# The low parts of the weights: one place modulo 512 bytes in the feature-major product, another in the token-major one

## The chip, the cores and the metric

The kernel runs on one core of one Trainium2 chip. The metric is the device time of one execution in microseconds (us). Before the change it is 2848.39 us, the median of 3 runs (2848.35 to 2848.42).

## The reference

A two-layer network over one sequence of 256 tokens with 2048 features, in float32. Layer 0 mixes tokens with a gated recurrence (HGRN2, 8 heads) and with low-rank attention (MLA, 8 heads); layer 1 mixes with retention (8 heads of 256 by 512). After each mixer come a gated feed-forward part with a short convolution, and a gated embedding of a second input `p`. Cut to its frame:

```python
for i in range(DEPTH):                                   # 2
    u = rmsnorm(h, norm_mix[i])
    mix = even_mixer(u, ...) if i % 2 == 0 else odd_mixer(u, ...)
    h = h + mix
    h = h + conv_ffn(rmsnorm(h, norm_ffn[i]), w_gate, w_up, conv_w, conv_b, w_down)   # 2048 -> 5632 -> 2048
    gate = sigmoid(rmsnorm(h, norm_ple[i]) @ ple_w_gate[i])
    h = h + (p[i] @ ple_w_proj[i]) * gate
```

Nearly all the work is products of an activation of 256 tokens with float32 weight matrices, each of which is used once: about 520 MB of weights are read.

## The kernel before

**Two parts of a number.** The products are made in the type float32r. To keep float32's accuracy, each operand is split into a high part (rounded to float32r) and a low part (the remainder): weights into `wh` and `wl`, activations into the two halves of one tile `x` of 128 partitions by 512 numbers, `x[:, 0:256]` high and `x[:, 256:512]` low, for 256 tokens. A product is the sum of three: `wh` with x high, `wh` with x low, `wl` with x high.

**The weights' way.** A block of weights of 128 partitions by 1024 numbers (512 KB) comes by DMA into `raw` (line 153, 4 buffers). ScalarE rounds it into `wh` (line 158, 3 buffers); VectorE subtracts and writes `wl` (line 161, 4 buffers).

**The feature-major product**, `gemm_fm` (line 172): the output's features lie on the partitions. A slice of 128 by 128 weights is loaded into TensorE, and x streams past it: once for `wh` with both halves of x, 512 columns (line 184), once for `wl` with the high half, 256 columns (line 186). The weights of two blocks are taken together (`RUN = 2`): 16 matmuls with `wh`, then the 16 with `wl` for the same chunks. `gemm_fm1` (line 199) does the same in matmuls of 256 columns (lines 209, 211, 212), one after the other for each slice.

**The token-major product**, `gemm_tm` (line 217): tokens lie on the partitions. Here 128 by 128 numbers of x are loaded, and 512 columns of weights stream past: x high with `wh` (line 228), x high with `wl` (line 229), x low with `wh` (line 230), for two halves of the tokens. `first_values` (line 235) is the same for the first weights of the kernel (lines 263 to 265); its first two chunks have buffers of their own, `wh0` and `wl0`.

In both forms one operand stands still in the array (it is loaded by an instruction of its own, which the profile shows as PEld and which runs beside the matmul ahead of it), and the other streams. In the feature-major form the low part of a weight is loaded; in the token-major one it streams.

**Where tiles lie.** Pools hand out a partition's bytes in the order of allocation. A tile of 512 or 1024 numbers takes 2048 or 4096 bytes, so all buffers of one kind lie at the same place modulo 512, and so does each slice of 128 numbers within them. `shift` (line 141) puts a small unused tile ahead of a pool's tiles to move them. Before the change the x tiles of every stage, `raw` and `wh` lie at 64 modulo 512, and `wl`, behind a pad of `LOW_SHIFT` = 320 bytes, at 384. `wh0` and `wl0` of `first_values` lie at 0.

**Order.** Python generators (`spawn`, `pump`) interleave the small work of each stage with the products: a product's loop calls `pump()` after a block or two, which lets every waiting stage issue its next step. Each engine then runs its instructions in the order in which they were issued, and waits on semaphores where data or a buffer is missing.

**The rotary part of the queries** is one such stage: `q_rope` in `mla` (line 803) writes y (tag `ly`, 2 buffers), its square, y times a gain into `lyg` (line 810, 1 buffer), and `rotate` (line 769) multiplies that with a permutation on TensorE (line 772). It runs twice.

Of the kernel before, what the change touches and what calls it, by code (L numbers as in the profile page):

```python
# [8 lines left out]
F32 = mybir.dt.float32  # L9
F32R = mybir.dt.float32r  # L10
BF16 = mybir.dt.bfloat16
I32 = mybir.dt.int32
AF = mybir.ActivationFunctionType
# [4 lines left out]
P = 128  # L18
T = 256
# [5 lines left out]
F_HALVES = ((0, 24), (24, 44))  # L25
KB = 4
RUN = 2
LOW_SHIFT = 320
EPS = 1e-6

HG_HEADS = 8
# [47 lines left out]
def hybrid_kernel(ctx, tc, io):  # L79
    nc = tc.nc  # L80
# [4 lines left out]
    xpool = ctx.enter_context(tc.tile_pool(name="xpool", bufs=NX, reuse_waits="tile"))  # L85
    wpool = ctx.enter_context(tc.tile_pool(name="wpool", bufs=4))
# [18 lines left out]
    def vcol(name, i=0, n=1):  # L105
        if name == "mix0":
            return vec0[:, i:i + n]
        a = VEC[name][0] + i
        return vec[:, a:a + n]
# [7 lines left out]
    def pump():  # L117
        for g in active[:]:
            if next(g, active) is active:
                active.remove(g)  # L120
# [17 lines left out]

    shifted = set()

    def shift(pool, name, n):


        if name not in shifted:
            shifted.add(name)
            pool.tile([P, n // 4], F32, name=f"pad_{name}", bufs=1)

    def load_w(src, width):
        return split_w(fetch_w(src, width), width)

    def fetch_w(src, width):
        raw = wpool.tile([P, width], F32, tag="raw", name="raw", bufs=4)
        nc.sync.dma_start(out=raw, in_=src)
        return raw

    def split_w(raw, width):
        wh = wpool.tile([P, width], F32R, tag="wh", name="wh", bufs=3)
        nc.scalar.copy(wh, raw)  # L158
        shift(wpool, "wl", LOW_SHIFT)
        wl = wpool.tile([P, width], F32R, tag="wl", name="wl", bufs=RUN + 2)  # L160
        nc.vector.tensor_tensor(wl, raw, wh.bitcast(F32), op=ALU.subtract)  # L161
        return wh, wl

    def blocks_of(blocks, n, width, kb, sub=None):

        sub = sub or kb
        for k0 in range(0, n, sub):
            k1 = min(n, k0 + sub)
            o = (k0 % kb) * width
            yield range(k0, k1), load_w(blocks[k0 // kb][:, o:o + (k1 - k0) * width], (k1 - k0) * width)  # L170

    def gemm_fm(blocks, xs):

# [43 lines left out]
    def gemm_tm(blocks, xs, sub=None):  # L217

        ps = [psum.tile([P, 512], F32, tag="mm", name="mm", bufs=5) for _ in range(2)]
        n = len(xs)  # L220
        for ks, (wh, wl) in blocks_of(blocks, n, 512, 2, sub):
            for kc in ks:
                x = xs[kc]
                o = (kc - ks[0]) * 512
                for m in range(2):
                    xh = x[:, m * P:(m + 1) * P]
                    xl = x[:, T + m * P:T + (m + 1) * P]
                    nc.tensor.matmul(ps[m], xh, wh[:, o:o + 512], start=(kc == 0), stop=False)  # L228
                    nc.tensor.matmul(ps[m], xh, wl[:, o:o + 512], start=False, stop=False)  # L229
                    nc.tensor.matmul(ps[m], xl, wh[:, o:o + 512], start=False, stop=(kc == n - 1))  # L230
            if ks[-1] % 4 == 3:
                pump()
        return ps

    def first_values(src, xs):


        ps = [[psum.tile([P, 512], F32, tag="mm", name="mm", bufs=5) for _ in range(2)] for _ in range(2)]
        n = len(xs)
        with tc.tile_pool(name="first", bufs=4) as first:  # L240
            raws = {}

            def fetch(kc):
                if kc < 2:
                    for g in range(2):
                        raws[kc, g] = first.tile([P, 512], F32, tag="raw0", name="raw0")
                        nc.sync.dma_start(out=raws[kc, g], in_=src[kc][:, g * 512:(g + 1) * 512])
                elif kc < n:
                    raws[kc] = fetch_w(src[kc], 1024)

            def split_half(raw):
                wh = first.tile([P, 512], F32R, tag="wh0", name="wh0")
                nc.scalar.copy(wh, raw)
                wl = first.tile([P, 512], F32R, tag="wl0", name="wl0")
                nc.vector.tensor_tensor(wl, raw, wh.bitcast(F32), op=ALU.subtract)
                return wh, wl

            def products(kc, g, wh, wl, o):
                x = xs[kc]
                for m in range(2):  # L260
                    xh = x[:, m * P:(m + 1) * P]
                    xl = x[:, T + m * P:T + (m + 1) * P]
                    nc.tensor.matmul(ps[g][m], xh, wh[:, o:o + 512], start=(kc == 0), stop=False)  # L263
                    nc.tensor.matmul(ps[g][m], xh, wl[:, o:o + 512], start=False, stop=False)  # L264
                    nc.tensor.matmul(ps[g][m], xl, wh[:, o:o + 512], start=False, stop=(kc == n - 1))  # L265

            xs.fetch(0, 0)
            fetch(0)
            xs.fetch(0, 1)
            fetch(1)  # L270
            for i in range(1, 3):
                xs.fetch(i)
                fetch(2 * i)
                fetch(2 * i + 1)
            xs.fetch(3)
            for kc in range(n):
                if kc < 2:
                    for g in range(2):
                        products(kc, g, *split_half(raws[kc, g]), 0)
                else:  # L280
                    wh, wl = split_w(raws[kc], 1024)
                    for g in range(2):
                        products(kc, g, wh, wl, g * 512)
                    fetch(kc + 4)
                    if kc % 2 == 0 and kc // 2 + 3 < n // 2:
                        xs.fetch(kc // 2 + 3)
                if kc % 4 == 3:
                    pump()
        return ps
# [126 lines left out]
    rope_t = {}  # L416

    def rope_tables(tpool):
        posi = tpool.tile([P, T], I32, tag="posi", name="posi", bufs=1)
        nc.sync.dma_start(out=posi, in_=io["positions"])  # L420
        yield from steps(2)
        posf = tpool.tile([P, T], F32, tag="posf", name="posf", bufs=1)
        nc.vector.tensor_copy(posf, posi)
        for name in ("mla", "ret"):
            ang = tpool.tile([P, T], F32, tag="ang", name="ang", bufs=1)
            nc.vector.tensor_scalar(ang, posf, vcol(f"invf_{name}"), None, op0=ALU.mult)
            cs = cpool.tile([P, T], F32, name=f"cos_{name}")
            sn = cpool.tile([P, T], F32, name=f"sin_{name}")
            sin_of(sn, ang, 0.0, tpool)
            sin_of(cs, ang, 0.25, tpool)  # L430
            rope_t[name] = (cs, sn)
            yield


    def ffn_and_ple(i, st):
        rs = token_stats(st[0], D, 2)
        xs = st[1]
        cw, cb = f"cw{i}", f"cb{i}"
        st = new_norm()
        with tc.tile_pool(name=f"ffn{i}", bufs=2, reuse_waits="tile") as fp:  # L440
            silu = {}

            def gate(ps, f):
# [46 lines left out]
            xs = st[1]  # L490
# [174 lines left out]
    def even_mixer(rs, xs):  # L665
# [1 line left out]
        mix_a, mix_b = {}, {}  # L667
        first = first_values(io["w_hv"], xs)
        with tc.tile_pool(name="low", bufs=2) as low:
            shift(low, "low", 64)  # L670
            kpe = low.tile([P, 1, T], F32, name="kpe", bufs=1)
            with tc.tile_pool(name="l0a", bufs=2) as pool:
                hvs = {}
# [91 lines left out]
    def mla(pool, kpe, ckv, cq, rkv, rqa, mix, fill):  # L765
# [3 lines left out]
        def rotate(dst, y):  # L769
            ps = small([P, 2, T], "sm_rot")  # L770
            n = y.shape[1]
            nc.tensor.matmul(ps[:, 0:n], mcol("swap"), y, start=True, stop=True)
            mul(y, y, bcast(cos, n), nc.gpsimd)
            mul(dst, ps[:, 0:n], bcast(sin, n))
            nc.vector.tensor_tensor(dst, dst, y, op=ALU.add)
# [25 lines left out]
        qr, sqr, mv, pairs = {}, {}, {}, {}  # L801

        def q_rope(ps, g):
            yield from until(rqa, "bc")
            y = pool.tile([P, 2, T], F32, tag="ly", name="ly")
            mul(y, ps, bcast(rqa["bc"]))
            sq = pool.tile([P, 2, T], F32, name=f"sqr{g}", bufs=1)
            nc.scalar.activation(sq, y, AF.Square)
            yg = pool.tile([P, 2, T], F32, tag="lyg", name="lyg", bufs=1)
            nc.scalar.activation(yg, y, AF.Copy, scale=vcol("qr"))  # L810
            yield
            z = pool.tile([P, 2, T], F32, name=f"qr{g}", bufs=1)
            rotate(z, yg)
            for j in range(2):
                sqr[2 * g + j] = sq[:, j]
                qr[2 * g + j] = z[:, j]
# [111 lines left out]
    def odd_mixer(st):  # L928
        rs = token_stats(st[0], D, 2)
        xs = st[1]  # L930
        st = new_norm()
        cs, sn = rope_t["ret"]
        with tc.tile_pool(name="l1", bufs=1, reuse_waits="tile") as l1, \
                tc.tile_pool(name="l1t", bufs=2, reuse_waits="tile") as lt:
            shift(l1, "l1", 64)
            mx = {}
            rot = {}
            gates = {}
# [146 lines left out]
    xs = Arriving()  # L1085
# [120 lines left out]
```

## Time and profile before

| | |
|---|---|
| time, median of 3 runs | 2848.39 us |
| profiled execution, its own time | 2848.95 us |
| its span, first to last instruction | 2847.1 us |
| VectorE busy | 1898.6 us (67%) |
| ScalarE busy | 1403.0 us (49%) |
| DMA queue of the weights | 522.95 MB, 57.5% of 16 engines |

A row of the timeline gives the start in us from the span's start, the time to the end of the last instruction of the group, the engine (PE is TensorE's matmuls, PEld its weight loads), the line of the kernel, the operation, what it writes and reads, and after an x how many instructions stand in the group. Matmuls are pipelined: one starts long before the one ahead of it has ended. What a stream of them costs is therefore the **step**, from one start to the next start, and not the duration of one. A group's mean step is the start of the next group, less its own start, divided by its count.

### The profile page before, as it was taken

The page shows a single profiled execution, that of the slowest core. Times are in us where ns is not written, and L with a number is a line of the kernel's source. Part 1 is how long each engine was busy: PE and PEld are TensorE (multiplying, and loading weights), DVE is VectorE, ACT ScalarE, POOL GpSimd, SP SyncE. Part 2 cuts the span into 40 slices and gives each one's busy share as a digit, 9 for nine tenths or more (in the row PEclk, how much of TensorE's full clock was granted, in tenths as well). Part 3 has the DMA queues.
Part 4 walks back from the last instruction along what each step waited for, and adds up shares of the span by engine and source line. Part 5 has one row for each costly group of instructions (what it writes and reads, how often), then busy time and mean ns, then how long its engine had stood idle before and what let it go on. Part 6 is the DMA issues. An engine that isn't in the chain of part 4 may idle for free.

```text
span 2847.1 us, 41083 instructions
## 1 busy us (share of the span) xinstructions
PE 2838.5 (100%) x16025; PEld 2474.0 (87%) x16025; DVE 1898.6 (67%) x2753; ACT 1403.0 (49%) x1844; POOL 84.7 (3%) x123
## 2 busy tenths in 40 slices
PE   9999999999999999999999999999999999999999
PEld 7888888888888888888888888888888888888888
DVE  8776787766557776785555555556777755777666
ACT  6665555444344444564444444445444433444444
POOL 1110300000000000000000000000000000000000
PEclk9999999999999999999999999999999999999999
DMA  7555445556655665565555555555665655666564
GB/s 242 175 157 163 133 154 189 188 191 192 192 187 191 189 189 188 187 194 183 182 180 182 189 185 181 178 178 185 196 191 186 193 189 189 192 188 194 186 194 165
DMA packets 147939, 525.58 MB, mean 185 GB/s; under 512 B 16544, under 2 KB 18336, under 8 KB 147744
## 3 DMA queue, kind: packets, MB, share of 16 engines
q1 hardware_dynamic: 147600, 522.95, 57.5%
q8 instruction: 125, 2.05, 0.3%
q14 instruction: 70, 0.57, 0.1%
q10 hardware_dynamic: 144, 0.01, 0.0%
HBM read 520.80 MB, written 2.10 MB: 184 GB/s over the span
## 4 chain that ended last, share of the span: by engine, by line
PE 98%; DVE 1%; DMA 0%; POOL 0%; issue 0%; ACT 0%; SPq 0%; DVEq 0%
PE mm L184 52%; PE mm L186 27%; PE mm L230 4%; PE mm L229 4%; PE mm L228 4%; PE sm_ro L1008 1%; PE mm L209 1%; PE mm L212 1%; PE mm L211 1%; PE mm L264 0%; PE mm L265 0%; PE sm_ra L987 0%; PE mm L263 0%; DMA raw<-in_w_hv 0%; PE sm_sc L875 0%; DVE wl L161 0%
## 5 line engine op out<-in xcount | busy, mean ns | idle before, releaser
L161 DVE TENSOR_TENSOR wl<-raw,wh 128x1024 fp32r<-128x1024 f32 (+1 forms) x990 | 1200.4, 1219 | 819.3 <-ACT wh L158 801.6
L158 ACT CAST wh<-raw 128x1024 fp32r<-128x1024 f32 (+1 forms) x990 | 1032.0, 1043 | 1205.2 <-PE mm L184 776.7
L184 PE MATMUL mm<-xs,wh 128*128 128x512 f32 x4288 | 1028.8, 391 | 0.0
L184 PEld LDWEIGHTS mm<-xs,wh 128*128 128x128 f32 x4288 | 787.1, 188 | 153.1 <-DVE xs L311 0.4
L186 PEld LDWEIGHTS mm<-xs,wl 128*128 128x128 f32 x4288 | 541.2, 189 | 19.1
L186 PE MATMUL mm<-xs,wl 128*128 128x256 f32 x4288 | 550.5, 281 | 0.0
L184 PE MATMUL mm<-hs,wh 128*128 128x512 f32 x1408 | 337.2, 391 | 0.0
L184 PEld LDWEIGHTS mm<-hs,wh 128*128 128x128 f32 x1408 | 258.2, 188 | 49.6
L229 PE MATMUL mm<-wl,xs 128*128 128x512 f32 x512 | 202.0, 394 | 0.0
L230 PE MATMUL mm<-wh,xs 128*128 128x512 f32 x512 | 201.8, 394 | 0.0
L228 PE MATMUL mm<-wh,xs 128*128 128x512 f32 x512 | 201.7, 394 | 0.0
L186 PEld LDWEIGHTS mm<-hs,wl 128*128 128x128 f32 x1408 | 179.4, 189 | 7.3
L186 PE MATMUL mm<-hs,wl 128*128 128x256 f32 x1408 | 181.7, 281 | 0.0
L295 ACT COPY evt<-mm 128x256 f32<-128x256 f32 x300 | 98.2, 374 | 92.9 <-PE mm L186 92.9
L184 PE MATMUL mm<-xo,wh 128*128 128x512 f32 x512 | 122.7, 391 | 0.0
L230 PEld LDWEIGHTS mm<-wh,xs 128*128 128x128 f32 x512 | 96.2, 188 | 22.4
L229 PEld LDWEIGHTS mm<-wl,xs 128*128 128x128 f32 x512 | 96.1, 188 | 22.1
L228 PEld LDWEIGHTS mm<-wh,xs 128*128 128x128 f32 x512 | 96.2, 188 | 21.9
L184 PEld LDWEIGHTS mm<-xo,wh 128*128 128x128 f32 x512 | 94.0, 188 | 18.5 <-DVE xo L1025 0.3
L399 DVE TENSOR_TENSOR h<-h,mm 128x256 f32<-128x256 f32 x128 | 48.1, 415 | 35.7 <-PE mm L186 35.7
L186 PEld LDWEIGHTS mm<-xo,wl 128*128 128x128 f32 x512 | 64.9, 189 | 2.4
L186 PE MATMUL mm<-xo,wl 128*128 128x256 f32 x512 | 65.9, 281 | 0.0
(275 smaller groups left out, 1952.5 us busy)
## 6 DMA issues: line engine op xcount, KB each, us to landing
raw<-in_wg SPq DMA_DIRECT2D x176, 512.0 KB, 3.7
raw<-in_wu SPq DMA_DIRECT2D x176, 512.0 KB, 4.1
raw<-in_wd SPq DMA_DIRECT2D x176, 512.0 KB, 3.9
raw<-in_w_oqk SPq DMA_DIRECT2D x64, 512.0 KB, 4.2
raw<-in_w_ov SPq DMA_DIRECT2D x64, 512.0 KB, 3.7
raw<-in_w_og SPq DMA_DIRECT2D x64, 512.0 KB, 3.5
raw<-in_w_oo SPq DMA_DIRECT2D x64, 512.0 KB, 4.1
raw<-in_wpg SPq DMA_DIRECT2D x60, 512.0 KB, 3.6
```

Source lines behind the costliest of these rows:

```text
L158: nc.scalar.copy(wh, raw)
L161: nc.vector.tensor_tensor(wl, raw, wh.bitcast(F32), op=ALU.subtract)
L184: nc.tensor.matmul(ps[j], w[:, o:o + P], xs[kc], start=(kc == 0), stop=False)
L186: nc.tensor.matmul(ps[j][:, 0:T], w[:, o:o + P], xs[kc][:, 0:T], start=False, stop=(kc == n - 1))
L209: nc.tensor.matmul(ps[:, j], w, x[:, 0:T], start=(kc == 0 and j == 0), stop=False, skip_group_check=True)
L211: nc.tensor.matmul(ps[:, j], w, x[:, T:2 * T], start=False, stop=False, skip_group_check=True)
L212: nc.tensor.matmul(ps[:, j], wl[:, o:o + P], x[:, 0:T], start=False, stop=(kc == n - 1 and j == ncol - 1), skip_group_check=True)
L228: nc.tensor.matmul(ps[m], xh, wh[:, o:o + 512], start=(kc == 0), stop=False)
L229: nc.tensor.matmul(ps[m], xh, wl[:, o:o + 512], start=False, stop=False)
L230: nc.tensor.matmul(ps[m], xl, wh[:, o:o + 512], start=False, stop=(kc == n - 1))
L295: nc.scalar.copy(tmp[:, j], ps[j][:, T:2 * T])
L399: nc.vector.tensor_tensor(h[i][:, j], h[i][:, j], ps[j][:, 0:T], op=ALU.add)
```

## The change

The tile of a low part grows by 128 numbers (512 bytes), and the part lies in it at one of two places: 48 numbers (192 bytes) from its start in the feature-major product, at its start in the token-major one. The pad ahead of `wl` is gone, so the tile starts at 64 modulo 512. Low parts are thus at 256 modulo 512 in the feature-major product (and in `gemm_fm1`) and at 64 in the token-major one (and in `first_values` from its third chunk on); they were at 384 in all. The pads of the other pools are given anew so that x tiles and `wh` stay at 64 in every stage. Some tiles that no product of weights reads move too: `acc` and `sq` from 384 to 64, `evt` from 192 to 384. `wh0` and `wl0` move from 0 to 192.

The four larger tiles take 2048 bytes more and the dropped pad gives 320 back. To make room, `posi` shares the buffer of `ang`, and `lyg` goes: y is scaled in its own buffer.

```diff
-LOW_SHIFT = 320
+LOW_AT = {"features": 48, "tokens": 0}
+PADS = {"xs": 0, "wh": 0, "low": 384, "ret": 384, "ffn": 320}
...
-    def split_w(raw, width):
+    def split_w(raw, width, form):
+
+        shift(wpool, "wh")
         wh = wpool.tile([P, width], F32R, tag="wh", name="wh", bufs=3)
         nc.scalar.copy(wh, raw)
-        shift(wpool, "wl", LOW_SHIFT)
-        wl = wpool.tile([P, width], F32R, tag="wl", name="wl", bufs=RUN + 2)
+        wl = wpool.tile([P, 1024 + 128], F32R, tag="wl", name="wl", bufs=RUN + 2)
+        wl = wl[:, LOW_AT[form]:LOW_AT[form] + width]
         nc.vector.tensor_tensor(wl, raw, wh.bitcast(F32), op=ALU.subtract)
...
-        for ks, (wh, wl) in blocks_of(blocks, n, 512, 2, sub):
+        for ks, (wh, wl) in blocks_of(blocks, n, 512, 2, sub, "tokens"):
...
-                    wh, wl = split_w(raws[kc], 1024)
+                    wh, wl = split_w(raws[kc], 1024, "tokens")
...
-        posi = tpool.tile([P, T], I32, tag="posi", name="posi", bufs=1)
+        posi = tpool.tile([P, T], I32, tag="ang", name="posi", bufs=1)
...
-            yg = pool.tile([P, 2, T], F32, tag="lyg", name="lyg", bufs=1)
-            nc.scalar.activation(yg, y, AF.Copy, scale=vcol("qr"))
+            nc.scalar.activation(y, y, AF.Copy, scale=vcol("qr"))
             yield
             z = pool.tile([P, 2, T], F32, name=f"qr{g}", bufs=1)
-            rotate(z, yg)
+            rotate(z, y)
```

No product changes its instructions, their order or their shapes. The one place where instructions change places is the second run of `q_rope`. On TensorE, in the small products of the attention's low-rank part (`x_kva` and `x_qa` are their activations, `sm_rot` the permuted queries), there stands before:

```order
597 L211 MATMUL mm<-x_kva_2431,wh 128x256
598 L212 MATMUL mm<-x_kva_2431,wl 128x256
599 L209 MATMUL mm<-x_qa_2630,wh 128x256
600 L211 MATMUL mm<-x_qa_2630,wh 128x256
601 L212 MATMUL mm<-x_qa_2630,wl 128x256
602 L209 MATMUL mm<-x_qa_2630,wh 128x256
603 L772 MATMUL sm_rot<-lyg,mat 128x512
604 L211 MATMUL mm<-x_qa_2630,wh 128x256
```

and now:

```order
597 L217 MATMUL mm<-x_kva_2430,wh 128x256
598 L218 MATMUL mm<-x_kva_2430,wl 128x256
599 L779 MATMUL sm_rot<-ly,mat 128x512
600 L215 MATMUL mm<-x_qa_2629,wh 128x256
601 L217 MATMUL mm<-x_qa_2629,wh 128x256
602 L218 MATMUL mm<-x_qa_2629,wl 128x256
603 L215 MATMUL mm<-x_qa_2629,wh 128x256
604 L217 MATMUL mm<-x_qa_2629,wh 128x256
```

The permutation stands four matmuls earlier. On VectorE, at the same place, there stands before:

```order
274 L161 TENSOR_TENSOR wl<-raw,wh 128x1024
275 L775 TENSOR_TENSOR qr_2987<-qr_2987,lyg 128x512
276 L302 TENSOR_TENSOR ly<-mm,rbc 128x512
277 L161 TENSOR_TENSOR wl<-raw,wh 128x1024
278 L302 TENSOR_TENSOR qr_3030<-sm_rot,sin_mla 128x512
279 L775 TENSOR_TENSOR qr_3030<-qr_3030,lyg 128x512
```

and now:

```order
274 L166 TENSOR_TENSOR wl<-raw,wh 128x1024
275 L782 TENSOR_TENSOR qr_2985<-qr_2985,ly 128x512
276 L308 TENSOR_TENSOR ly<-mm,rbc 128x512
277 L308 TENSOR_TENSOR qr_3027<-sm_rot,sin_mla 128x512
278 L166 TENSOR_TENSOR wl<-raw,wh 128x1024
279 L782 TENSOR_TENSOR qr_3027<-qr_3027,ly 128x512
```

The second product with the sine has changed places with the subtraction that makes a block's low part.

More of the change, by code (lines that the diff above doesn't have):

```diff
@@ L139, in hybrid_kernel, with shift, load_w @@
     shifted = set()
-    def shift(pool, name, n):
-        if name not in shifted:
+    def shift(pool, name):
+        if name not in shifted and PADS[name[:3]]:
             shifted.add(name)
-            pool.tile([P, n // 4], F32, name=f"pad_{name}", bufs=1)
-    def load_w(src, width):
-        return split_w(fetch_w(src, width), width)
+            pool.tile([P, PADS[name[:3]] // 4], F32, name=f"pad_{name}", bufs=1)
+    shift(xpool, "xs")
+    def load_w(src, width, form):
+        return split_w(fetch_w(src, width), width, form)
     def fetch_w(src, width):
@@ L154, in fetch_w, with blocks_of @@
         return raw
-    def split_w(raw, width):
+    def split_w(raw, width, form):
+        shift(wpool, "wh")
         wh = wpool.tile([P, width], F32R, tag="wh", name="wh", bufs=3)
         nc.scalar.copy(wh, raw)
-        shift(wpool, "wl", LOW_SHIFT)
-        wl = wpool.tile([P, width], F32R, tag="wl", name="wl", bufs=RUN + 2)
+        wl = wpool.tile([P, 1024 + 128], F32R, tag="wl", name="wl", bufs=RUN + 2)
+        wl = wl[:, LOW_AT[form]:LOW_AT[form] + width]
         nc.vector.tensor_tensor(wl, raw, wh.bitcast(F32), op=ALU.subtract)
         return wh, wl
-    def blocks_of(blocks, n, width, kb, sub=None):
+    def blocks_of(blocks, n, width, kb, sub=None, form="features"):
         sub = sub or kb
@@ L169, in blocks_of @@
             o = (k0 % kb) * width
-            yield range(k0, k1), load_w(blocks[k0 // kb][:, o:o + (k1 - k0) * width], (k1 - k0) * width)
+            yield range(k0, k1), load_w(
+                blocks[k0 // kb][:, o:o + (k1 - k0) * width], (k1 - k0) * width, form)
     def gemm_fm(blocks, xs):
@@ L440, in ffn_and_ple @@
         with tc.tile_pool(name=f"ffn{i}", bufs=2, reuse_waits="tile") as fp:
+            shift(fp, f"ffn{i}")
             silu = {}
@@ L669, in even_mixer @@
         with tc.tile_pool(name="low", bufs=2) as low:
-            shift(low, "low", 64)
+            shift(low, "low")
             kpe = low.tile([P, 1, T], F32, name="kpe", bufs=1)
@@ L934, in odd_mixer @@
                 tc.tile_pool(name="l1t", bufs=2, reuse_waits="tile") as lt:
-            shift(l1, "l1", 64)
+            shift(l1, "ret")
             mx = {}
```

## The prediction

> **What bounds the kernel now.** First the page: how much of the span TensorE works, at which clock, and who is on the chain that ended last.
>
> ```profile
> span 2847.1 us, 41083 instructions
> PE 2838.5 (100%) x16025; PEld 2474.0 (87%) x16025; DVE 1898.6 (67%) x2753; ACT 1403.0 (49%) x1844; POOL 84.7 (3%) x123
> ...
> PEclk9999999999999999999999999999999999999999
> ...
> PE 98%; DVE 1%; DMA 0%; POOL 0%; issue 0%; ACT 0%; SPq 0%; DVEq 0%
> PE mm L184 52%; PE mm L186 27%; PE mm L230 4%; PE mm L229 4%; PE mm L228 4%; PE sm_ro L1008 1%; PE mm L209 1%; PE mm L212 1%; PE mm L211 1%; PE mm L264 0%; PE mm L265 0%; PE sm_ra L987 0%; PE mm L263 0%; DMA raw<-in_w_hv 0%; PE sm_sc L875 0%; DVE wl L161 0%
> ```
>
> TensorE's matmuls are the chain, at full clock throughout. The second view, the waits of TensorE, leaves nothing else to gain: its longest is the first below, and six more are under 1 us each.
>
> ```profile
> PE spin L99 <- DVE cold L96: 1.1, 1, 1.1
> ...
> PE sm_rot L772 <- ACT lyg L810: 0.6, 1, 0.6
> ```
>
> So the time is the number of matmuls times their steps. The third view gives the numbers. Only the matmuls that read a low part change; the rows of lines 186, 212, 229 and 264:
>
> ```profile
> L186 PE MATMUL mm<-xs,wl 128*128 128x256 f32 x4288 | 550.5, 281 | 0.0
> L229 PE MATMUL mm<-wl,xs 128*128 128x512 f32 x512 | 202.0, 394 | 0.0
> ...
> L186 PE MATMUL mm<-hs,wl 128*128 128x256 f32 x1408 | 181.7, 281 | 0.0
> ...
> L186 PE MATMUL mm<-xo,wl 128*128 128x256 f32 x512 | 65.9, 281 | 0.0
> ...
> L264 PE MATMUL mm<-wl,xs 128*128 128x512 f32 x64 | 25.6, 401 | 0.7 <-DVE wl L161 0.4 <-DVE wl L255 0.2
> ...
> L212 PE MATMUL mm<-xs,wl 128*128 128x256 f32 x80 | 22.6, 282 | 0.0
> ...
> L186 PE MATMUL mm<-xa,wl 128*128 128x256 f32 x128 | 16.6, 283 | 0.0
> L186 PE MATMUL mm<-xb,wl 128*128 128x256 f32 x128 | 16.4, 281 | 0.0
> ...
> L212 PE MATMUL mm<-x_qa,wl 128*128 128x256 f32 x48 | 13.5, 282 | 0.0
> ...
> L186 PE MATMUL mm<-px,wl 128*128 128x256 f32 x64 | 10.2, 281 | 0.0
> ...
> L212 PE MATMUL mm<-x_kva,wl 128*128 128x256 f32 x32 | 9.0, 282 | 0.0
> ...
> L229 PE MATMUL mm<-wl,x_kva 128*128 128x512 f32 x16 | 6.4, 401 | 0.3 <-DVE wl L161 0.3
> ```
>
> The feature-major low products are 4288 + 1408 + 512 + 128 + 128 + 64 = 6528, or 408 groups of 16 (each beside as many matmuls of line 184). The token-major ones are 3 x (512 + 16) + 3 x 64 = 1776.
>
> **The steps, from the timeline.** Fourth, the two forms side by side in layer 1, where both stand within 15 us:
>
> ```profile
> 1467.31 0.39 PE L230 MATMUL mm<-wh,xs 128*128 128x512 f32 x1
> ...
> 1470.79 0.39 PE L230 MATMUL mm<-wh,xs 128*128 128x512 f32 x1
> ...
> 1475.63 2.20 PE L1008 MATMUL sm_ro<-rv,rat 128*128 128x512 f32 x9
> 1477.67 1.97 PE L184 MATMUL mm<-xs,wh 128*128 128x512 f32 x8
> 1479.48 2.05 PE L186 MATMUL mm<-xs,wl 128*128 128x256 f32 x16
> 1481.37 3.14 PE L184 MATMUL mm<-xs,wh 128*128 128x512 f32 x13
> ```
>
> From the first row to the second are 15 steps, so a token-major matmul costs 3.48 / 15 = 232.0 ns. Line 1008, also of 512 columns, costs 2.04 / 9 = 226.7, and line 184 costs 1.81 / 8 = 226.3: the same shape, 5.3 ns cheaper. In both cheap cases the loaded and the streamed operand lie at 64 modulo 512. In the token-major form every third matmul streams from 384. A low product of 256 columns costs 1.89 / 16 = 118.1 here, with its loaded weights at 384.
>
> The fifth view is one whole pair of groups in a feed-forward part:
>
> ```profile
> 702.00 3.81 PE L184 MATMUL mm<-hs,wh 128*128 128x512 f32 x16
> ...
> 703.16 0.61 PE L184 MATMUL mm<-hs,wh 128*128 128x512 f32 x2
> ...
> 705.65 2.05 PE L186 MATMUL mm<-hs,wl 128*128 128x256 f32 x16
> 707.54 0.63 PE L184 MATMUL mm<-hs,wh 128*128 128x512 f32 x2
> ```
>
> (The second row is the sixth matmul of the first.) After the low products ahead of them, the first five high products take 1.16 / 5 = 232 ns, the other eleven 2.49 / 11 = 226.4. So a change from one place to the other costs about 1.16 - 5 x 0.2267 = 0.027 us, and then the stream settles. The low group never does: 1.89 / 16 = 118.1.
>
> Yet the low product can be cheaper with the very same places. In layer 0, behind some small matmuls of the recurrence:
>
> ```profile
> 106.23 1.64 PE L186 MATMUL mm<-xs,wl 128*128 128x256 f32 x13
> 107.71 2.00 PE L184 MATMUL mm<-xs,wh 128*128 128x512 f32 x8
> ```
>
> 1.48 / 13 = 113.8 ns. What matters is thus a place and how the stream was entered; 118.1 is not the shape's own price.
>
> **The change, part by part.** *Token-major.* With the low parts at 64, all that streams and all that is loaded lies at 64, as on lines 1008 and 184. I take their settled 226.7 in place of 232.0: 1776 x 5.3 ns = 9.4 us, less an entry of 0.027 us for each of some 18 calls, 0.5: **9 us less**. Bounds: 9.4, and 0 if the 232.0 belongs to the form.
>
> *Feature-major.* With the loaded low parts at 256 the trace has no row: counted round 512, a load at 384 lies 192 behind the stream's 64, one at 256 lies 192 ahead of it, and nothing ties the two together. From below: settled at once at 113.8, and the following high group spared its entry, (118.1 - 113.8) x 16 = 0.069, plus 0.027, is 0.096 us a pair: 39 us less. From above: the other pair of places that the trace shows, in the first two chunks of `first_values`, where 0 streams and 64 is loaded:
>
> ```profile
> 9.74 0.39 PE L263 MATMUL mm<-wh,xs 128*128 128x512 f32 x1
> ...
> 11.61 0.39 PE L265 MATMUL mm<-wh,xs 128*128 128x512 f32 x1
> ```
>
> Eight steps, 1.87 / 8 = 233.8, which is 7.1 over settled. On 6528 low products at 118.1 it would be 46 us more; over the settled 113.8 only 2.8 ns more than now, 18 us. Between these I take the behaviour of the high groups, the nearest row: an entry of 0.027 us, then settled. That is 0.069 - 0.027 = 0.042 us a group, and 408 x 0.042 = **17 us less**. I choose this because both settled cases (226.7 and 113.8) are reached after a few steps in this trace; it is a choice, and half of it is open.
>
> *`gemm_fm1`* has 80 + 48 + 32 = 160 low products among 480 of 256 columns. Two of its high ones in layer 0, 24 steps apart:
>
> ```profile
> 283.02 0.28 PE L211 MATMUL mm<-x_qa,wh 128*128 128x256 f32 x1
> ...
> 285.85 0.28 PE L211 MATMUL mm<-x_qa,wh 128*128 128x256 f32 x1
> ```
>
> 2.83 / 24 = 117.9. Settled at 113.8 they would give 480 x 4.1 ns = 2 us, and as much could be lost. I take 0.
>
> *Room.* `posi` in the buffer of `ang` and y scaled in place add no instruction. The permutation of the queries (line 772), four matmuls earlier, is at most 4 x 0.118 = 0.5 us nearer to the scaling that it waited 0.6 us for; what it loses in waiting stands behind it as work, and the wait for `lyg` to come free is gone. VectorE's next product into `ly` stands behind the sum that frees the buffer, on the same engine, so it waits for nothing new. Between 0.6 less and 0.5 more; I take 0.
>
> *Cover.* If TensorE runs 1% faster, the weights must come faster. VectorE, which makes the low parts, waits long:
>
> ```profile
> L161 DVE TENSOR_TENSOR wl<-raw,wh 128x1024 fp32r<-128x1024 f32 (+1 forms) x990 | 1200.4, 1219 | 819.3 <-ACT wh L158 801.6
> ...
> q1 hardware_dynamic: 147600, 522.95, 57.5%
> ```
>
> 819 us of idle time, and a queue at 57.5%, hide 1 to 2% easily; without that cover the gain would stop at VectorE's 1219 ns a block, while TensorE takes 8 x (228.1 + 118.1) ns = 2.77 us for a block (228.1 is 3.65 / 16 of the pair above).
>
> Sum against the profiled execution's 2848.95 us (span 2847.1 and 1.85 around it): 9 + 17 = 26 less, 2823. The median of the runs is 0.56 lower, so 2848.4 - 26 = **2822 us**.
>
> **A rule that speaks against it.** The Trainium skill, "TensorE: Matmul & The Clock Gate", section "Step-by-step: what each phase is for", says that TensorE has two independent read ports of SBUF and that "Loading the next tile's weights doesn't steal SBUF read bandwidth from the running matmul." By that rule places are indifferent and the time stays at 2848. The rows of 226.7 and 232.0 for one shape do not agree with it, unless the difference comes from the form.
>
> **Rivals.**
>
> 1. *The low products stay at 118* whatever their place, since they are loaded without a pause between two loads: only the token-major gain stays, 2848.4 - 9 = 2839 us. For it: the 118 holds in `gemm_fm1` too, where high slices at 64 are loaded between. Against it: 113.8.
> 2. *Everything settles at once*: 9 + 39 = 48 less, 2800 us. For it: the high stream stays settled for eleven steps. Against it: each high group pays its entry, even after the cheap low group (107.71 to the next row would show it).
> 3. *Slower*: at 256 the loads meet the stream of x at a worse moment, in each low product. At the 2.8 ns worked out above it costs 18, with the token-major gain 9 more: 2857; at 7.1 ns, 46 - 9 = 37 more, 2885. It decides from 9 us / 6528 = 1.4 ns, that is from a step of 119.5.
> 4. *Places do nothing*: steps of 232.0 and 118.1 belong to the forms and their order, not to addresses; the text then moves tiles and no time: 2848. For it: one set of places has both 118.1 and 113.8. Against it: 226.7 and 232.0 in the same microseconds. The page named above would have this one.
>
> **How the numbers follow.** Forecast 0.31 (2807 to 2834), rival 1 0.28, rival 2 0.15, rival 3 0.16, rival 4 with gains that cancel 0.10. A measurement of this kernel tells about 0.2% (5.7 us) from no change. Faster by more than that are the forecast, rival 2 and nearly all of rival 1: 0.72; within it 0.12; slower 0.16. The range goes from rival 2 with the 2 us of `gemm_fm1` beside it, 2798, past rival 1 to the token-major gain with 7 of its 9 us lost again, 2846; it leaves out rival 3 and half of rival 4, 0.16 + 0.05.
>
> **What would show it.** Token-major steps at 226.7 from the sixth matmul of a call on, line 186's groups at 1.84 us for 16 in place of 1.89, the first five of line 184 still near 232, waits of TensorE under 5 us in all. A low group above 1.91 us proves me wrong in sign; one at 1.89 leaves rival 1.

## The result, and the profile after

The change makes the kernel a little slower: 2853.01 us against 2848.54 us, both medians of 22 runs, a ratio of 1.0016 (95% interval 1.0009 to 1.0022). The forecast was 2822 us. The profiled execution has a span of 2851.1 us, against 2847.1.

The page of the changed kernel looks like the one of before: TensorE is the chain, at full clock. Of the shares by line, only that of line 190 has moved, by one per cent (line 190 is the former 184, 192 the former 186, 234 to 236 the former 228 to 230):

```profile
span 2851.1 us, 41084 instructions
PE 2843.7 (100%) x16025; PEld 2472.3 (87%) x16025; DVE 1898.1 (67%) x2753; ACT 1403.4 (49%) x1844; POOL 84.3 (3%) x123
...
PE mm L190 53%; PE mm L192 27%; PE mm L235 4%; PE mm L236 4%; PE mm L234 4%; PE mm L215 1%; PE mm L217 1%; PE mm L218 1%; PE sm_ro L1014 1%; PE sm_ra L993 0%; PE mm L270 0%; PE mm L271 0%; PE mm L269 0%; DMA raw<-in_w_hv 0%; DVE wl L166 0%; PE sm_sc L881 0%
```

The high feature-major products have 53% of the chain where they had 52%, though no operand of theirs was moved. The waits of TensorE are as short as before, and the one for `lyg` is gone:

```profile
PE spin L100 <- DVE cold L97: 1.1, 1, 1.1
PE sm_bc L353 <- DVE dg L345: 0.6, 1, 0.6
PE mm L270 <- DVE wl L166: 0.5, 2, 0.3
PE mm L235 <- DVE wl L166: 0.3, 1, 0.3
PE sm_col L367 <- DVE lacc L364: 0.2, 1, 0.2
```

So the time lies in the steps again. The timeline of the changed kernel at the place in layer 1 that the prediction used (start in us first; the group's count at the end):

```profile
1466.05 0.39 PE L236 MATMUL mm<-wh,xs 128*128 128x512 f32 x1
...
1469.44 0.39 PE L236 MATMUL mm<-wh,xs 128*128 128x512 f32 x1
...
1475.79 1.98 PE L190 MATMUL mm<-xs,wh 128*128 128x512 f32 x8
1477.61 2.20 PE L1014 MATMUL sm_ro<-rv,rat 128*128 128x512 f32 x9
```

Fifteen token-major steps take 3.39 us, 226.0 ns each at this resolution; over all of `gemm_tm` the trace has a mean of 227.1, and 232.0 before (steps of 260 ns and more, at starts and breaks, left out). The token-major part of the change does what was forecast. The high group right behind it, 1.82 / 8 = 227.5, pays no entry (the longer steps at a group's start); it paid none before either, where the same group takes 1.82 us.

The pair of groups in the feed-forward part:

```profile
706.53 2.05 PE L192 MATMUL mm<-hs,wl 128*128 128x256 f32 x16
708.41 3.85 PE L190 MATMUL mm<-hs,wh 128*128 128x512 f32 x16
...
710.74 0.61 PE L190 MATMUL mm<-hs,wh 128*128 128x512 f32 x2
...
712.10 1.10 PE L192 MATMUL mm<-hs,wl 128*128 128x256 f32 x8
```

The low group still takes 1.88 us for 16, 117.5 ns a step. The third row begins with the eleventh matmul of the high group: its first ten steps take 2.33 / 10 = 233.0 ns, the other six 1.36 / 6 = 226.7. Before, five steps were long, and the group took 3.65 us; now ten are, and it takes 3.69.

Averaged step by step over the 358 groups of 16 that follow a low group undisturbed, the steps of the high group in ns are:

| step | 1 | 2 | 3 | 4 | 5 | 6 | 7 | 8 | 9 | 10 | 11 to 15 |
|---|---|---|---|---|---|---|---|---|---|---|---|
| before | 233.1 | 235.9 | 228.4 | 232.5 | 230.8 | 226.7 | 226.6 | 226.7 | 226.7 | 226.6 | 226.7 |
| after | 240.7 | 237.4 | 233.4 | 235.6 | 224.3 | 230.9 | 235.6 | 228.4 | 232.4 | 230.7 | 226.7 |

The last four long steps of after (235.6, 228.4, 232.4, 230.7) are steps 2 to 5 of before. So the rows can be read as one sequence of steps, which lasts until the stream settles, and after the change the group enters it five steps earlier.

The sum, with means over the groups of each trace (high 3.6533 to 3.6887 us, low 1.8864 to 1.8840), is 408 x 0.0354 = 14.4 us more, 408 x 0.0024 = 1.0 less, and 1776 x 4.9 ns = 8.7 less, together 4.7 us more. Measured is 2853.01 - 2848.54 = 4.5. Not all groups are whole ones, so this is an estimate. Added up step by step over the two traces, line 190 takes 13.6 us more, line 192 takes 0.2 less, `gemm_tm` 7.7 less, `first_values` 1.1 less, `gemm_fm1` 0.8 less and the rest 0.3 more: 4.0 us, which is the difference of the two spans.

### The profile page after: what moved, and what is told of

Same layout as the page of the kernel before. It is cut to its first block, busy times and chain, and to the rows that moved or that the text cites. A ratio compares the mean times of both kernels' runs of the same rounds, so it can differ in the third digit from the quotient of the medians.

```text
span 2851.1 us, 41084 instructions
## 1 busy us (share of the span) xinstructions
PE 2843.7 (100%) x16025; PEld 2472.3 (87%) x16025; DVE 1898.1 (67%) x2753; ACT 1403.4 (49%) x1844; POOL 84.3 (3%) x123
## 4 chain that ended last, share of the span: by engine, by line
PE 98%; DVE 1%; DMA 0%; SPq 0%; POOL 0%; ACT 0%; issue 0%
PE mm L190 53%; PE mm L192 27%; PE mm L235 4%; PE mm L236 4%; PE mm L234 4%; PE mm L215 1%; PE mm L217 1%; PE mm L218 1%; PE sm_ro L1014 1%; PE sm_ra L993 0%; PE mm L270 0%; PE mm L271 0%; PE mm L269 0%; DMA raw<-in_w_hv 0%; DVE wl L166 0%; PE sm_sc L881 0%
```

## The experiments

All are the changed kernel with the constants below altered. The kernel of before, run beside each batch, gave medians of 2848.56 to 2848.63 us, so times of different batches can be compared.

**One part alone.** First the token-major part alone, then the feature-major part alone.

```diff
-LOW_AT = {"features": 48, "tokens": 0}
+LOW_AT = {"features": 80, "tokens": 0}      # e1: 384 and 64
+LOW_AT = {"features": 48, "tokens": 80}     # e2: 256 and 384
```

> As the changed kernel, but the feature-major low parts back at 384 modulo 512 (80 numbers into their tile); token-major ones stay at 64. Theory P (the place of the loaded low part decides how the following high group enters): the high groups enter again in five steps (16 take 3.653 us, not 3.689), low groups 1.887, token-major steps stay near 227: 2853.0 - 408 x (3.689 - 3.653 - 0.003) us = 2839.5 us, below both kernels. Rival S (what lengthened the entry is something else that the change moved: the wider low tiles, the small tiles, y scaled in place): the high groups still take ten steps and 3.689 us, 2853 us.

> As the changed kernel, but the token-major low parts back at 384; feature-major ones stay at 256. Theory P: the token-major step returns to 232.0 ns (plus 9 us), the high groups keep 3.689 us: 2862 us. Rival S (token-major gain comes from something else in the change): step stays at 227, 2853 us.

Measured were 2839.36 us for e1 (0.9968 of before, 0.9955 to 0.9980) and 2860.56 us for e2 (1.0043, 1.0029 to 1.0057). The timeline of e1 in the feed-forward part:

```profile
704.09 2.05 PE L192 MATMUL mm<-hs,wl 128*128 128x256 f32 x16
705.98 3.82 PE L190 MATMUL mm<-hs,wh 128*128 128x512 f32 x16
709.63 2.05 PE L192 MATMUL mm<-hs,wl 128*128 128x256 f32 x16
711.52 2.68 PE L190 MATMUL mm<-hs,wh 128*128 128x512 f32 x11
```

and of e2:

```profile
703.09 3.85 PE L190 MATMUL mm<-hs,wh 128*128 128x512 f32 x16
706.78 2.05 PE L192 MATMUL mm<-hs,wl 128*128 128x256 f32 x16
708.66 3.85 PE L190 MATMUL mm<-hs,wh 128*128 128x512 f32 x16
712.35 1.81 PE L192 MATMUL mm<-hs,wl 128*128 128x256 f32 x14
```

With the feature-major low parts at 384 the high group is back at 3.65 us, with all else of the change in place; at 256 it takes 3.69 whether or not the token-major part was moved. The wider tiles, the moved small tiles and the scaling in place are out as the cause of the longer entry (rival S). With all else of the change in place, the feature-major place costs 2853.01 - 2839.36 = 13.7 us, and the token-major place gains 2860.56 - 2853.01 = 7.6. The two parts nearly add up: 2839.36 + 2860.56 - 2853.01 = 2846.9, where before is at 2848.5. The 1.6 us between are what both runs hold of the change besides the two places, so the 9.2 us that e1 gains on before are not the token-major place alone. The changed kernel with both low parts back at 384, which would show these 1.6 us by themselves, was not run.

**All at one place, and a row of places.** If the long steps came from the change of place between `wl` and `wh`, they would vanish with all at 64 (e3).

```diff
-LOW_AT = {"features": 48, "tokens": 0}
+LOW_AT = {"features": 0, "tokens": 0}       # e3: 64
+LOW_AT = {"features": 64, "tokens": 0}      # e4: 320
+LOW_AT = {"features": 32, "tokens": 0}      # e5: 192
+LOW_AT = {"features": 16, "tokens": 0}      # e6: 128
+LOW_AT = {"features": 88, "tokens": 0}      # e7: 416
+LOW_AT = {"features": 72, "tokens": 0}      # e8: 352
```

> All low parts at 64, as x and the high parts. Theory P1 (an entry is paid because the loaded place changes from the low parts' to the high parts'): no entry at all, 16 high matmuls take 3.627 us and low ones may settle at 113.3: 2839.5 - 408 x 0.026 = 2829 us, down to 2800 if the low ones settle. Rival P2 (the entry comes from the change of shape, 256 to 512 columns, with loads back to back before it; the place only shifts where the stream enters): an entry remains, 3.65 to 3.69 us, low steps at 118: 2839 to 2854 us.

> Feature-major low parts at 320, token-major at 64. One of a row of places. Theory P: low groups stay at 424 cycles of 0.833 ns for three (117.8 ns a step) and the high group enters the same fixed run of steps (289, 285, 280, 283, 269, 277, 283, 274, 279, 277 cycles, then 272) at another point: between 3.627 us (none) and 3.689 us (all ten), 2829 to 2854 us. Rival S: 2853 us whatever the place.

> Feature-major low parts at 192, token-major at 64. 64 and 320 gave the same steps to the cycle, so the place seems to count modulo 256; of the places 0, 64, 128 and 192 modulo 256 only this one is not measured. Theory M (modulo 256): a fourth pattern of its own, with token-major steps at 227; from the three known ones the low group lies between 1.884 and 1.913 us and the high one between 3.653 and 3.689: 2839 to 2865 us. Rival L (low products settle at the right place): low groups at 16 x 113.3 = 1.813 us, 2839.4 - 408 x 0.072 = 2810 us.

> Feature-major low parts at 128, token-major at 64. Theory M (the place counts modulo 256): the same as at 384, low groups 1.887, high groups 3.653 us, 2839.4 us. Rival (modulo 512): another pattern, 2839 to 2865 us.

> Feature-major low parts at 416, half way between two multiples of 64 (160 modulo 256), token-major at 64. If the place counts in lines of 64 bytes, a load that starts inside one touches nine lines in place of eight, and the steps change from both neighbours; if it counts only which line comes first, they equal those at 384: 2839.4 us. Between 2810 (all settled) and 2865.

> Feature-major low parts at 352 (96 modulo 256), between 320 and 384, token-major at 64. The same question as at 416: equal to 320 if only the line counts (2852 us), to 384 if the next one (2839 us), or a pattern of its own, between 2810 and 2865.

The table gives the measured times, with the means over the groups of 16 in each trace; token-major low parts lie at 64 in every row. Each trace is of one execution, which lies within 2.4 us of the median beside it.

| feature-major low parts at | modulo 256 | low group, us | high group, us | time, us |
|---|---|---|---|---|
| 256 (the change) | 0 | 1.8840 | 3.6887 | 2853.01 |
| 64 (e3) | 64 | 1.9125 | 3.6549 | 2851.44 |
| 320 (e4) | 64 | 1.9125 | 3.6549 | 2851.95 |
| 352 (e8) | 96 | 1.8916 | 3.6789 | 2852.89 |
| 128 (e6) | 128 | 1.8848 | 3.6533 | 2838.96 |
| 384 (e1) | 128 | 1.8852 | 3.6533 | 2839.36 |
| 416 (e7) | 160 | 1.8775 | 3.6555 | 2838.94 |
| 192 (e5) | 192 | 1.9238 | 3.6436 | 2851.15 |

The timeline of e3:

```profile
701.92 2.08 PE L192 MATMUL mm<-hs,wl 128*128 128x256 f32 x16
703.83 3.82 PE L190 MATMUL mm<-hs,wh 128*128 128x512 f32 x16
707.49 2.08 PE L192 MATMUL mm<-hs,wl 128*128 128x256 f32 x16
```

and of e5:

```profile
703.39 3.81 PE L190 MATMUL mm<-hs,wh 128*128 128x512 f32 x16
707.03 2.08 PE L192 MATMUL mm<-hs,wl 128*128 128x256 f32 x16
708.96 3.81 PE L190 MATMUL mm<-hs,wh 128*128 128x512 f32 x16
```

In e3, where all operands lie at 64, the low group takes 1.91 us and the high one still 3.66: an entry of the same five steps, without any change of place. So a change of place is not what makes the entry. What is left is the switch from groups of 256 columns to groups of 512 (rival P2): the high group behind `gemm_tm`, which has 512 columns too, paid none. The place of the low parts shifts where the stream enters. At 64 the low products themselves get slower, 1.9125 / 16 = 119.5 ns. In e5 the high group has two long steps at its start and one at its end, the shortest of all, and the low group is the slowest, 120.2 ns: 11.8 us over e1 by 408 x (0.0386 - 0.0097), and 11.8 measured.

No place tried makes the low products of a feed-forward part settle at 113.3 (rival L). Yet at 384 they do run so elsewhere. One group in layer 0, in the kernel of before and then in e1:

```profile
112.27 2.05 PE L186 MATMUL mm<-xs,wl 128*128 128x256 f32 x16
114.15 2.00 PE L184 MATMUL mm<-xs,wh 128*128 128x512 f32 x8
...
112.07 1.98 PE L192 MATMUL mm<-xs,wl 128*128 128x256 f32 x16
113.88 2.00 PE L190 MATMUL mm<-xs,wh 128*128 128x512 f32 x8
```

At one and the same place, behind eight high products in both kernels, it takes 1.88 us before and 1.81 in e1. Six groups of e1 run at 113.3 ns, each behind a high group of 8. What lets them is not shown.

The equal rows for 64 and 320, and for 128 and 384, show that here the place counts modulo 256, not 512, so the change's 256 should be the same as 0, which was not run. Theory M said so for 128. By time, 352 lies with 320 and 416 with 384; by their groups the places 96 and 160 differ from both neighbours, so within this range places finer than 64 bytes count too. The sequence stays the same: in e8 the steps 2 to 9 of the high group are the steps 3 to 10 of the change (233.4, 234.9, 224.8, 230.7, 234.9, 228.2, 231.9 and 230.4 ns). In every run x and `wh` lie at 64, so the runs do not tell whether the place of the low part counts or its distance from the others.

e7 has the quickest low groups, yet its time does not differ from that of e1 and e6: by the groups it would be 408 x 0.0055 = 2.2 us less than e1, and it is 0.4. Its single runs go from 2837.85 to 2841.27 us, and the traced one, the longest, holds a wait of 2.0 us for a low part in `first_values`. Differences of this size are not settled here.

**The streamed operand.**

```diff
-LOW_AT = {"features": 48, "tokens": 0}
+LOW_AT = {"features": 80, "tokens": 64}     # e11: 384 and 320
```

> Feature-major low parts at 384, token-major ones at 320 in place of 64. Theory M (places count modulo 256 for the streamed operand too): token-major step 227 ns, 2839.4 us. Rival (modulo 512 for what streams): the step goes towards 232, up to 2848 us.

Measured were 2838.95 us and a token-major step of 226.9 ns, as with 64. For this pair of places, what streams counts modulo 256 too.

**The price of a switch.** With `RUN = 1` the low products follow each block, in groups of 8, and there are twice as many switches.

```diff
-RUN = 2
+RUN = 1       # e9: with the change; e10: with the places of e1
```

> The changed kernel (feature-major low parts at 256) with RUN = 1: low products after each block, in groups of 8, so twice as many entries of high groups. Theory E (an entry is paid once per switch from low to high products, as the same run of steps): the first eight steps cost 1.866 us where eight settled ones cost 1.813, so 816 x 0.053 = 43 us in place of 408 x 0.062 = 25.5: 2853 + 17.6 = 2870 us. Rival C (the long steps belong to a place in the block's time, such as its weights arriving or VectorE's writing, and not to the switch): about 2853 us.

> Low parts at 384 and 64 (the best so far) with RUN = 1. Theory E: entry of five steps, 0.0276 us, paid 816 times in place of 408, and the low group's last step is longer by 0.0025 twice as often: 2839.4 + 11.3 + 1 = 2852 us. Rival C: 2839 us.

Measured were 2848.28 us for e10, 8.9 more than e1, where 12 were expected and none by rival C. Its timeline:

```profile
702.88 2.00 PE L190 MATMUL mm<-hs,wh 128*128 128x512 f32 x8
704.71 1.11 PE L192 MATMUL mm<-hs,wl 128*128 128x256 f32 x8
```

The high groups of 8 in its trace have a mean of 1.8375 us, and 408 x (2 x 1.8375 - 3.6533) = 8.9. The switch is what is paid for, and rival C falls.

e9 came out at 2860.72 us, 7.7 more than the change and not 17.6, and its single runs spread from 2851.23 to 2869.01, where all others stay within 5 us. The trace is of the shortest of its eight runs, that of 2851.23:

```profile
703.62 1.99 PE L190 MATMUL mm<-hs,wh 128*128 128x512 f32 x8
705.44 1.10 PE L192 MATMUL mm<-hs,wl 128*128 128x256 f32 x8
706.38 2.02 PE L190 MATMUL mm<-hs,wh 128*128 128x512 f32 x8
708.24 1.11 PE L192 MATMUL mm<-hs,wl 128*128 128x256 f32 x8
709.18 1.99 PE L190 MATMUL mm<-hs,wh 128*128 128x512 f32 x8
711.01 1.10 PE L192 MATMUL mm<-hs,wl 128*128 128x256 f32 x8
```

High groups of 8 take 1.82 and 1.86 us in turn: in this run two entries, one late and one early in the sequence, alternate. That accounts for this run, not for the median; the longer ones left no trace, and what makes e9 fall on different times from run to run is not shown. Theory E's price per switch was roughly right for e10 and failed for e9.

That the place alone does not fix the entry can be seen in the changed kernel itself, at one spot in layer 1:

```profile
1934.00 1.98 PE L192 MATMUL mm<-xo,wl 128*128 128x256 f32 x16
1935.82 3.81 PE L190 MATMUL mm<-xo,wh 128*128 128x512 f32 x16
1939.47 2.05 PE L192 MATMUL mm<-xo,wl 128*128 128x256 f32 x16
```

The low parts lie at 256 here as everywhere, but this low group takes 1.82 us in place of 1.88, and the high group behind it 3.65 in place of 3.69: the entry of before. How the low group ran counts, and not only where its weights lie. What sets that is not shown.

## Why the prediction was wrong

- **What bounds the kernel** was right: TensorE's steps and nothing else, before and after, with waits under 4 us in all. In the traces of the variants they are under 6 us in all.
- **Token-major, 9 us less**: right. The step went from 232.0 to 227.1 ns, 8.7 us by the forecast's count, and the place alone gains 7.6 us by the runs (e2 against the change). The row to draw on was the settled 512-column stream with both operands at 64. The 1776 are all token-major products and not only those that read a low part, but 232.0 is the mean over all of them, so the sum holds.
- **Feature-major, 17 us less**: this is the step that failed. It was said that a low group pays an entry and then settles near 113.8, as the high groups settle. It does not: 117.8 ns a step at 256 (1.8840 / 16) as at 384, and 119.5 and 120.2 at the other two multiples of 64. The 113.8 of the trace of before is real, but it was reached behind the small matmuls of the recurrence; behind the whole high groups of a feed-forward part no place tried reaches it. The rows had said so: 16 steps without settling, in groups all over the kernel. Summed over the traces, line 192 gained 0.2 us, and the whole feature-major place cost 13.7 us.
- **The entry of the high group**, 0.027 us, was held constant, or gone at best (rival 2). It rose to 0.062 us (3.6887 less 16 x 0.22667), 14.4 us over the kernel by the group means (13.6 by the sum over the traces), more than the token-major gain. This is the term that turned the sign. The upper bound of the feature-major part was drawn for the low products' own steps; that they could lengthen the steps of a stream that was not touched was in none of the rivals. Rival 1 (low products stay at 118) had the low products right. Its 2839 us is what e1 measures, in part by luck: e1 holds 1.6 us of gain that are not the token-major place. The sign set down for this rival, a low group at 1.89 us, came true (1.88), but it looked at the low group alone and could not see the entry.
- **Slower, rival 3**, had the sign and the place of the change right, and the wrong mechanism: the low step did not rise.
- **`gemm_fm1` and the room made** at 0: nearly right. `gemm_fm1` takes 0.8 us less in the trace of the change and 0.7 less in e1, where its low parts lie at 384 as before, so this is not the place. The wait of 0.6 us for `lyg`, which stood among its matmuls and is gone, is about as large.
- **The Trainium skill's rule.** The Trainium skill ("TensorE: Matmul & The Clock Gate", "Step-by-step: what each phase is for") says that loading weights takes no read bandwidth from the running matmul. Read as the prediction read it, that places are indifferent, it does not agree with these operands: the same low products cost from 117.3 (1.8775 / 16) to 120.2 ns by where the loaded weights lie. Whether the loads take it from the matmul is not shown.

Why the sequence of steps is as it is, whether reads of the two operands meet in it, and why a step inside it can be shorter than a settled one (224.3 against 226.7 ns) stay open.

## What to carry to other kernels

A change that moves one operand of a stream can be paid for by the next stream: price the switch between two kinds of matmul apart from each kind's own step, in groups, on both sides of the switch. Two edits that were thought of as one should be run apart: here the token-major place gains 7.6 us, and the feature-major one costs 13.7 beside it. Where a settled step is taken from another context, look for one group that settles after the same neighbour before counting on it.

## What the runs showed of the hardware

- In these float32r streams a matmul's step depends on where its streamed operand and the weights loaded beside it lie, and that counts modulo 256 bytes for the pairs tried: 64 and 320, and 128 and 384, gave low groups equal to 0.4 ns in 1.88 us (loaded), and 64 and 320 token-major steps of 227.0 and 226.9 ns (streamed, e1 and e11).
- A high group of 512 columns behind a low group settles at 226.7 ns after up to ten steps of 224.3 to 240.7 ns. The runs at 256, 352 and 384 go through one sequence of steps from different points of it. Where a group enters depends on the low group ahead of it: at 256 the high group takes 3.69 us behind low groups of 1.88, and 3.65 behind the one of 1.82.
- Low groups of 256 columns repeat a pattern of three steps of 117.8 ns on average (256, 128 and 384), or run at 119.5 to 120.2 (64, 192), and stay there for the whole group; six groups of e1 run at 113.3 throughout.
